# First layer of a hybrid decoder trunk: the first four pairs of w_in tiles computed together, input features outermost

## The chip, the cores and the metric

The kernel runs on one core of one Trainium2 chip. The metric is the device time of one execution, in microseconds (us): the median of several runs of the same program. The engines are TensorE (PE for its matmuls, PEld for its weight loads), VectorE (DVE), ScalarE (ACT), GpSimd (POOL) and SyncE (SP), which issues nearly all transfers. "mm" below is one matmul instruction of 128 x 128 weights against 256 columns, unless another size is given.

## The reference, cut to what matters

Two layers; each has an RMSNorm, one input projection, three token mixers, gates, an output projection and a feed-forward part. The change touches only the start of layer 0: the norm and the first part of `h @ w_in`.

```python
def reference(x, mix_norm, w_in, ...):          # x (1, 256, 1024), w_in (2, 1024, 5892)
    for l in range(DEPTH):                       # DEPTH = 2
        h = _rmsnorm(x, mix_norm[l])
        proj = (h @ w_in[l]).astype(jnp.float32)
        ret_c, fox_c, rwkv_c, gate_c = jnp.split(proj, splits, axis=-1)
        ...
        y_rwkv = _rwkv7_branch(rwkv_c, ...)      # the first four pairs of tiles feed this branch
        ...
        x = x + merged @ w_out[l]
        ...
```

## The kernel before

Activations lie transposed: 128 input features on the partitions, 256 tokens along the row, so x is eight blocks of 128 x 256, loaded as four tiles `x0_0` to `x0_3` of two blocks each. A weight tile is 128 input features by 128 output features, and a **pair** is two output tiles: 2 x 8 weight blocks, one megabyte in `in_win`. All products are computed in two parts: a weight or an activation is split into a rounded part (`whi`, `xh`) and the rest (`wlo`, `xl`), and each block costs three mm: whi by xh, whi by xl, wlo by xh (`mm3`, L285 to L294). So a pair is 48 mm, and four pairs are 192.

**Weights.** `weights` lists the weight transfers in the order in which they are used. `_piece` (L251) takes the next one: SP transfers it into `raw` (three buffers), ACT makes `whi` of eight blocks (L273, a cast of 128 x 1024), DVE makes `wlo` (L274). `whi` and `wlo` have four buffers each; a transfer into `raw` waits until DVE has made the last `wlo` out of that buffer. `refill` stays some pieces ahead of TensorE.

**The start.** TensorE first runs 30 matmuls on a tile of zeros (`pz`, L170). SP issues x0_0, the parameters, half of the first weights, x0_1, the other half, x0_2, x0_3, then the second weights, the constants and so on. `norm_add` (L392, L393) scales each x tile by the norm's gain and splits it; the rest of the norm, one factor for each token, is applied to the results. `layer` calls it for all four x tiles, with pieces of weights between.

**The first four pairs.** `gemm_halves` with a cut of 7 computes pair 0 (all but the last input block of both tiles first), then `gemm_pair` computes pairs 1, 2 and 3, each over all eight input blocks before the next begins. The sum of squares (`norm_sum`, L403 to L407) ends in `rstd`, whose matmul `pn` (L419) stands between pairs 1 and 2 and whose small DVE chain leads to `dg`; `replicate` (matmul `pss`, L429) spreads the factor and stands between pairs 2 and 3. `rwkv_in` multiplies each pair by the factor (`pj`, L642), takes the difference of neighbouring tokens on POOL (`dd`, L644) and mixes (L633) into r, k, v and wg.

**After them.** Two generators, one of the matmuls and one of the RWKV steps, are interleaved by a table of weights (`PACE`); the scheduler orders each engine's instructions by priority. The next matmuls are `mqk` (L437 to L439, 48 of 512 columns) and `mv` (48 of 260 columns). The first RWKV step loads `lora` (L668, 256 KB), and the matmuls `pw` and `pa` (L673, L674) read it with `xw` (L663) and wg. Engines run their instructions in order.

Of the kernel before, what the change touches and what calls it, by code (L numbers as in the profile page):

```python
# [8 lines left out]
F32 = mybir.dt.float32  # L9
# [82 lines left out]
def pack_inputs(inp, depth=DEPTH):  # L92
    f = {k: np.asarray(v) for k, v in inp.items()}
    out = {}

    def fm(a, n):
        return a.reshape(n, P).T

    out["xt"] = np.ascontiguousarray(f["x"][0].T.reshape(KT, P, T).transpose(1, 0, 2))
    out["const"] = np.concatenate([CONSTS[k] for k in C_ORDER], 1)  # L100
    pr = []
    for l in range(depth):
        fb = np.broadcast_to(f["fox_f_bias"][l][None, :], (P, 4))
        cols = {
            "mixg": fm(f["mix_norm"][l], 8), "ffng": fm(f["ffn_norm"][l], 8), "mu": fm(f["rwkv_mu"][l], 8),
            "w0": fm(f["rwkv_w0"][l], 2), "a0": fm(f["rwkv_a0"][l], 2), "kk": fm(f["rwkv_k_k"][l], 2),
            "ka": fm(f["rwkv_k_a"][l], 2), "rk": fm(f["rwkv_r_k"][l], 2), "rgn": fm(f["rwkv_gn"][l], 2),
            "retgn": fm(f["ret_gn"][l], 2),
            "fq": np.tile(f["fox_q_norm"][l], 2)[:, None], "fk": np.tile(f["fox_k_norm"][l], 2)[:, None],
            "fb": fb, "w2a2": np.concatenate([f["rwkv_w2"][l], f["rwkv_a2"][l]], 0), "g2": f["rwkv_g2"][l],  # L110
        }
        pr.append(np.concatenate([cols[k] for k, _ in PARAMS], 1))
    out["par"] = np.ascontiguousarray(np.stack(pr))

    def tiles(w, cols, nk):
        return w[:, cols].reshape(nk, P, -1, P).transpose(1, 2, 0, 3)

    R, F, W, G = 0, 1024, 1024 + 772, 1024 + 772 + 1024
    order = np.concatenate([
        np.arange(W, W + 1024),  # L120
        np.arange(R, R + 512), np.arange(R + 768, R + 1024)])
    win, wqk, wv, wgt = [], [], [], []
    for l in range(depth):
        w = f["w_in"][l]
        t = tiles(w, order, KT)
        win.append(t.reshape(P, N_IN, 2, KT, P).transpose(1, 0, 2, 3, 4).reshape(N_IN, P, 2 * KT * P))
        wqk.append(w[:, F:F + 512].reshape(KT, P, 512).transpose(1, 0, 2).reshape(P, KT * 512))
        vf = w[:, F + 512:F + 772].reshape(KT, P, 260).transpose(1, 0, 2).reshape(P, KT * 260)
        vr = w[:, R + 512:R + 768].reshape(KT, P, 256).transpose(1, 0, 2).reshape(P, KT * 256)
        wv.append(np.concatenate([vf, vr], 1))  # L130
        wgt.append(tiles(w, np.arange(G, G + 3 * DM), KT).reshape(P, 3, 4, 2 * KT * P).transpose(1, 2, 0, 3))
    out["wqk"] = np.ascontiguousarray(np.stack(wqk))
    out["win"] = np.ascontiguousarray(np.stack(win))
    out["wgate"] = np.ascontiguousarray(np.stack(wgt))
    out["wv"] = np.ascontiguousarray(np.stack(wv))
    pp, wo, wg, wd = [], [], [], []
    for l in range(depth):
        pp.append(np.stack([tiles(f[n][l], np.arange(DM), 2).reshape(P, 2 * DM) for n in ("p_ret", "p_fox", "p_rwkv")]))
        wo.append(tiles(f["w_out"][l], np.arange(DM), KT).reshape(P, 4, 2 * KT * P).transpose(1, 0, 2))
        gu = tiles(f["w_gate_up"][l], np.arange(2 * DFF), KT).reshape(P, 2, FT // 2, 2 * KT * P)  # L140
        wg.append(gu.transpose(2, 1, 0, 3))
        wd.append(tiles(f["w_down"][l], np.arange(DM), FT).transpose(1, 0, 2, 3).reshape(4, 2, P, FT, P)
                  .transpose(0, 2, 1, 3, 4).reshape(4, P, 2 * FT * P))
    out["pp"] = np.ascontiguousarray(np.stack(pp))
    out["wo"] = np.ascontiguousarray(np.stack(wo))
    out["wg"] = np.ascontiguousarray(np.stack(wg))
    out["wd"] = np.ascontiguousarray(np.stack(wd))
    return out


class Kernel:
    def __init__(self, ctx, tc, d, depth=DEPTH, debug=None):
        self.tc, self.nc, self.d, self.depth = tc, tc.nc, d, depth
        self.debug = debug or {}
        nc = self.nc
        e = ctx.enter_context
        self.cp = e(tc.tile_pool(name="cp", bufs=1))
        self.raw = e(tc.tile_pool(name="raw", bufs=3))
        self.spl = e(tc.tile_pool(name="spl", bufs=4))
        self.xp = e(tc.tile_pool(name="xp", bufs=4))  # L160
        self.ps = e(tc.tile_pool(name="ps", bufs=4, space=bass.MemoryType.PSUM))
        self.dr = e(tc.tile_pool(name="dr", bufs=1, space=bass.MemoryType.DRAM))
        self.uid = 0


        zero = self.cp.tile([P, T], mybir.dt.bfloat16, name="zero")
        nc.vector.memset(zero, 0.0)
        pz = self.ps.tile([P, T], F32, tag="fr", bufs=2, name="pz")
        for _ in range(30):
            nc.tensor.matmul(pz, zero[:, 0:P], zero, start=True, stop=True)  # L170
        par = [self.cp.tile([P, P_RES], F32, name=f"par{l}") for l in range(depth)]

        self.pad(self.xp, 16)
        self.xt = [self.xp.tile([P, 2, T], F32, tag="x", bufs=5, name=f"x0_{j}") for j in range(4)]
        nc.sync.dma_start(self.xt[0], d["xt"][:, 0:2, :])
        nc.sync.dma_start(par[0], d["par"][0, :, 0:P_RES])
        self.jobs, self.raws, self.ready, self.cur = list(self.weights()), [], [], []
        w0 = self.raw.tile([P, 2080], F32, tag="raw", name=self.nm("raw"))
        for j in range(4):
            if j:  # L180
                nc.sync.dma_start(self.xt[j], d["xt"][:, 2 * j:2 * j + 2, :])
            if j < 2:
                nc.sync.dma_start(w0[:, 1024 * j:1024 * (j + 1)], d["win"][0, 0, :, 1024 * j:1024 * (j + 1)])
        self.jobs[0:1] = [(w0, 4, P, 0), (w0, 4, P, 4), (w0, 8, P, 8)]
        self.par = par
        self.con = con = self.cp.tile([P, C_RES], F32, name="con")
        self.identb, self.maskb = zero[:, 0:P], zero[:, P:]
        self.c = {}
        for k, (o, n) in C_OFF.items():
            if k in FETCHED:  # L190
                continue
            v = con[:, o:o + n]
            if k in C_SHAPE:
                v = v.rearrange("p (a b) -> p a b", a=C_SHAPE[k][0])
            self.c[k] = v
        cc = self.c["cc"]
        self.cc = lambda i: cc[:, i:i + 1]
# [24 lines left out]
    def weights(self):  # L222

        d = self.d
        for l in range(self.depth):
            for j in range(N_IN):
                yield d["win"][l, j], 16, P, 0
                if j == 3:
                    for k in (0, 4):
                        yield d["wqk"][l, :, k * 512:(k + 4) * 512], 4, 512, 0  # L230
                    yield d["wv"][l, :, 0:KT * 260], KT, 260, 0
            yield d["wv"][l, :, KT * 260:], KT, 256, 0
            for b in range(3):
                for c in range(4):
                    yield d["wgate"][l, b, c], 16, P, 0
                for bb in ((), (0, 1), (2,))[b]:
                    yield d["pp"][l, bb], 16, P, 0
            for j in range(4):
                yield d["wo"][l, j], 16, P, 0
# [68 lines left out]
    def gemm_halves(self, xs, kcut=None, hook=None, tag="mm"):  # L308
# [14 lines left out]
        for lo, hi in ((0, kcut), (kcut, n)):  # L323
# [3 lines left out]
            if hook and not lo:  # L327
                hook()
        return ps

    @staticmethod
    def run(gen):
# [130 lines left out]
    def layer(self, l):  # L463
        tc, nc, d = self.tc, self.nc, self.d
        if l == 0:
            self.norm_start(0, "mixg")
            for j in range(4):
                self.norm_add(j, False)
                if j != 2:
                    self.piece()  # L470
        xs = self.xs
        with ExitStack() as st:
            e = st.enter_context
# [22 lines left out]
    def mixers(self, l, xs):  # L496
        self.y = [None] * 3
        self.mx = []
        self.need = None
        ps = [self.gemm_halves(xs, 7, tag="rw")]  # L500
        if l == 0:
            self.load_rest()
        for _ in range(1):
            ps.append(self.run(self.gemm_pair(xs)))
        rn, dg = self.rstd()
        ps.append(self.run(self.gemm_pair(xs)))
        rstd = self.replicate(dg)
        rw = self.rwkv_in(l, xs, rstd, ps)
        clock = {"gemm": 0.0, "rwkv": 0.0}
        run = {"gemm": self.gemms(l, xs, rstd, rn), "rwkv": self.rwkv(l, rw)}  # L510
# [686 lines left out]
```

## Time and profile before

| | us |
|---|---|
| median of 3 runs (799.79 to 800.15) | 800.09 |
| the profiled execution's own time | 800.76 |
| its span, first to last instruction | 799.0 |
| TensorE busy with matmuls (7018 of them) | 783.6 (98%) |
| VectorE busy | 576.2 (72%) |
| ScalarE busy | 397.1 (50%) |
| GpSimd busy | 61.6 (8%) |

The span lies inside the profiled execution's time, which is 0.67 us above the median. A timeline row gives the start, the length, the engine, the line, the operation, output and inputs; matmuls overlap in the array, so the step from one start to the next is what one costs. A bracket at its end is the time that the engine stood idle before it, and what ended that.

### The profile page before, as it was taken

How to read it: one execution, taken by the hardware profiler on the slowest of the kernel's cores; microseconds unless marked ns; L12 is line 12 of the kernel's file. 1: busy time of each engine (PE TensorE's matmuls, PEld its weight loads, DVE VectorE, ACT ScalarE, POOL GpSimd, SP SyncE). 2: the span in 40 equal slices, each digit the busy share in tenths (PEclk: the TensorE clock that was granted, in tenths of full speed). 3: DMA queues.
4: the chain of work that ended last, by engine and by line, in shares of the span. 5: the costliest groups of instructions: out<-in, count | busy, mean ns of one | idle time of the engine just before them, and what ended most of it. 6: DMA issues, size and time to landing. Idle time of an engine off the chain costs nothing.

```text
span 799.0 us, 16543 instructions
## 1 busy us (share of the span) xinstructions
PE 783.6 (98%) x7018; PEld 762.5 (95%) x7018; DVE 576.2 (72%) x900; ACT 397.1 (50%) x543; POOL 61.6 (8%) x83
## 2 busy tenths in 40 slices
PE   8999899999999999999999999999999999999998
PEld 6999899999999999999998988999999999999997
DVE  5897979597867666656678798877878666666453
ACT  6367445535645444445444764554456545444331
POOL 3201210031000000000023030101110000000000
PEclk9999999999999999999999999999999999999999
DMA  8565524335454554556554553452445454555650
GB/s 308 208 226 167 170 80 169 140 114 205 161 208 167 203 205 172 191 184 211 200 188 175 197 172 106 162 174 106 142 176 190 180 201 174 206 202 164 211 190 27
DMA packets 27802, 140.42 MB, mean 176 GB/s; under 512 B 7600, under 2 KB 9168, under 8 KB 12496
## 3 DMA queue, kind: packets, MB, share of 16 engines
q1 hardware_dynamic: 27728, 139.36, 50.2%
q8 instruction: 55, 0.90, 0.5%
q14 instruction: 19, 0.16, 0.1%
HBM read 136.97 MB, written 1.33 MB: 173 GB/s over the span
## 4 chain that ended last, share of the span: by engine, by line
PE 88%; DVE 6%; DMA 2%; ACT 1%; issue 1%; POOL 1%; SPq 0%; POOLq 0%; DVEq 0%; ACTq 0%
PE mm L290 26%; PE mm L294 25%; PE mm L293 25%; DVE wlo L274 2%; PE mqk L439 1%; PE mqk L438 1%; PE mqk L437 1%; ACT whi L273 1%; DMA rsw<-rqk 1%; PE pgm L762 1%; DVE rkk L745 1%; DMA raw<-in_win 1%; DMA raw<-in_pp 1%; PE mv L437 1%; PE mv L439 1%
## 5 line engine op out<-in xcount | busy, mean ns | idle before, releaser
L273 ACT CAST whi<-raw 128x1024 fp32r<-128x1024 f32 (+1 forms) x257 | 264.7, 1033 | 321.7 <-PE mm L293 232.2
L274 DVE TENSOR_TENSOR wlo<-raw,whi 128x1024 fp32r<-128x1024 f32 (+1 forms) x257 | 313.3, 1221 | 143.0 <-ACT whi L273 142.3
L290 PE MATMUL mm<-xh,whi 128*128 128x256 f32 x1312 | 368.0, 280 | 0.5 <-ACT whi L273 0.5
L294 PE MATMUL mm<-xh,wlo 128*128 128x256 f32 x1248 | 346.3, 277 | 0.7 <-DVE wlo L274 0.7
L293 PE MATMUL mm<-xl,whi 128*128 128x256 f32 x1248 | 346.3, 278 | 0.0
L290 PEld LDWEIGHTS mm<-xh,whi 128*128 128x128 f32 x1312 | 246.6, 188 | 2.8 <-issue 0.9
L294 PEld LDWEIGHTS mm<-xh,wlo 128*128 128x128 f32 x1248 | 234.4, 188 | 1.1 <-DVE wlo L274 0.9
L293 PEld LDWEIGHTS mm<-xl,whi 128*128 128x128 f32 x1248 | 234.5, 188 | 0.8 <-issue 0.5
L290 PE MATMUL mm<-hi,whi 128*128 128x256 f32 x576 | 160.1, 279 | 0.0
L294 PE MATMUL mm<-hi,wlo 128*128 128x256 f32 x544 | 150.9, 277 | 0.0
L293 PE MATMUL mm<-lo,whi 128*128 128x256 f32 x544 | 150.8, 277 | 0.0
L290 PEld LDWEIGHTS mm<-hi,whi 128*128 128x128 f32 x576 | 108.2, 188 | 0.6 <-issue 0.3
L294 PEld LDWEIGHTS mm<-hi,wlo 128*128 128x128 f32 x544 | 102.1, 188 | 0.2
L293 PEld LDWEIGHTS mm<-lo,whi 128*128 128x128 f32 x544 | 102.1, 188 | 0.1
L569 POOL TENSOR_TENSOR gate<-gate,gate 128x512 f32<-128x512 f32 x10 | 13.3, 1336 | 142.3 <-DVE gate L567 142.3
L600 DVE TENSOR_TENSOR h<-t,mm 128x512 f32<-128x512 f32 x22 | 15.1, 687 | 11.5 <-PE mm L294 8.6
L567 DVE SCALAR_TENSOR_TENSOR gate<-gate,mm 128x512 f32<-128x512 f32 x24 | 16.1, 682 | 8.6 <-PE mm L294 8.5
L597 DVE TENSOR_TENSOR t<-mm,rstd 128x512 f32<-128x512 f32 (+1 forms) x24 | 15.2, 645 | 8.5 <-PE mm L294 8.5
L553 DVE TENSOR_TENSOR gate<-mm,rstd 128x512 f32<-128x512 f32 x24 | 16.5, 689 | 3.8 <-PE mm L294 3.5
L293 PE MATMUL mm<-xh,wlo 128*128 128x256 f32 x64 | 18.0, 281 | 0.7 <-DVE wlo L274 0.7
L439 PE MATMUL mv<-whi,xl 128*128 128x260 f32 (+1 forms) x64 | 18.6, 290 | 0.0
L437 PE MATMUL mv<-whi,xh 128*128 128x260 f32 (+1 forms) x64 | 18.6, 290 | 0.0
(259 smaller groups left out, 797.9 us busy)
## 6 DMA issues: line engine op xcount, KB each, us to landing
raw<-in_wg SPq DMA_DIRECT2D x44, 1024.0 KB, 4.7
raw<-in_wgate SPq DMA_DIRECT2D x24, 1024.0 KB, 4.8
raw<-in_wd SPq DMA_DIRECT2D x16, 1024.0 KB, 5.0
raw<-in_win SPq DMA_DIRECT2D x13, 1024.0 KB, 8.0
raw<-in_wo SPq DMA_DIRECT2D x8, 1024.0 KB, 4.8
raw<-in_pp SPq DMA_DIRECT2D x6, 1024.0 KB
raw<-in_wd SPq DMA_DIRECT2D x8, 768.0 KB, 4.3
raw<-in_wqk SPq DMA_DIRECT2D x4, 1024.0 KB, 5.0
```

The costliest lines, as they stand in the source:

```text
L273: nc.scalar.copy(hi[:, :m * width], r)
L274: nc.vector.tensor_tensor(out=lo[:, :m * width], in0=r, in1=hi[:, :m * width].bitcast(F32), op=ALU.subtract)
L290: nc.tensor.matmul(out, wh, xh, start=first, stop=False)
L293: nc.tensor.matmul(out, wh, xl, start=False, stop=False)
L294: nc.tensor.matmul(out, wl, xh, start=False, stop=last)
L437: nc.tensor.matmul(out, xh[:, s], wh, start=first, stop=False)
L439: nc.tensor.matmul(out, xl[:, s], wh, start=False, stop=last)
L553: nc.vector.tensor_tensor(out=g, in0=ps, in1=self.b2(rstd), op=ALU.mult)
L567: nc.vector.scalar_tensor_tensor(out=g, in0=g, scalar=1.0, in1=ps, op0=ALU.add, op1=ALU.mult)
L569: (nc.vector if bb == 2 and c >= 1 else nc.gpsimd).tensor_tensor(out=m, in0=m, in1=g, op=ALU.add)
L597: nc.vector.tensor_tensor(out=t[:, o, :], in0=p, in1=self.bs(rstd, o), op=ALU.mult)
L600: nc.vector.tensor_tensor(out=h, in0=t, in1=pu, op=ALU.mult)
```

## The change

The first four pairs of layer 0 get a function of their own, `first_pairs`. It holds four results at once (pairs 0 and 1 in the PSUM tiles of tag "rw", 2 and 3 in those of "mm") and goes over the input features in four steps kk of two blocks each; in each step it does all four pairs: 4 x 2 x 2 blocks, 48 mm. The weights of these pairs have a layout of their own, `win0`: one megabyte for each step kk, in the order of use. The other pairs stay in `win`.

Of the first megabyte, ScalarE's queue issues the first quarter (256 KB), ahead of the load of its activation table; SP issues x0_0, the parameters, the second quarter, the other half, then x0_1, the second megabyte, x0_2, the third, x0_3. The fourth megabyte and the constants follow. The x tile of step kk+1 is split while step kk is computed. `rstd` is called after pair 0 of the last step, `replicate` after pair 2 of the last step. The matmuls on zeros are 22 instead of 30. Layer 1 does what it did.

```diff
-        for _ in range(30):
+        for _ in range(22):
             nc.tensor.matmul(pz, zero[:, 0:P], zero, start=True, stop=True)
...
+        w = [self.raw.tile([P, 2080], F32, tag="raw", name=self.nm("raw")) for _ in range(3)]
+        nc.scalar.dma_start(w[0][:, 0:512], d["win0"][0, :, 0:512])
         nc.sync.dma_start(self.xt[0], d["xt"][:, 0:2, :])
         nc.sync.dma_start(par[0], d["par"][0, :, 0:P_RES])
-        w0 = self.raw.tile([P, 2080], F32, tag="raw", name=self.nm("raw"))
-        for j in range(4):
-            if j:
-                nc.sync.dma_start(self.xt[j], d["xt"][:, 2 * j:2 * j + 2, :])
-            if j < 2:
-                nc.sync.dma_start(w0[:, 1024 * j:1024 * (j + 1)], d["win"][0, 0, :, 1024 * j:1024 * (j + 1)])
-        self.jobs[0:1] = [(w0, 4, P, 0), (w0, 4, P, 4), (w0, 8, P, 8)]
+        nc.sync.dma_start(w[0][:, 512:1024], d["win0"][0, :, 512:1024])
+        nc.sync.dma_start(w[0][:, 1024:2048], d["win0"][0, :, 1024:2048])
+        for j in range(1, 4):
+            nc.sync.dma_start(self.xt[j], d["xt"][:, 2 * j:2 * j + 2, :])
+            if j < 3:
+                nc.sync.dma_start(w[j][:, 0:2048], d["win0"][j])
+        self.jobs[0:3] = [(w[0], 4, P, 0), (w[0], 4, P, 4), (w[0], 8, P, 8), (w[1], 16, P, 0), (w[2], 16, P, 0)]
...
+    def first_pairs(self, xs):
+        ps = [self.ps.tile([P, 2, T], F32, tag=t, bufs=n, name=self.nm("mm")) for t, n in (("rw", 2), ("rw", 2), ("mm", 4), ("mm", 4))]
+        for kk in range(4):
+            if kk < 3:
+                self.norm_add(kk + 1, False)
+            if kk == 2:
+                self.load_rest()
+            for j in range(4):
+                if kk == 3 and j == 1:
+                    rn, dg = self.rstd()
+                if kk == 3 and j == 3:
+                    rstd = self.replicate(dg)
+                for m in range(2):
+                    for k in range(2 * kk, 2 * kk + 2):
+                        if not self.cur:
+                            self.refill()
+                        self.mm3(ps[j][:, m, :], self.block(), xs[k], k == m == 0, k == KT - 1 and m == 1)
+        return ps, rn, rstd
...
             self.norm_start(0, "mixg")
-            for j in range(4):
-                self.norm_add(j, False)
-                if j != 2:
-                    self.piece()
+            self.norm_add(0, False)
+            self.piece()
...
-        ps = [self.gemm_halves(xs, 7, tag="rw")]
         if l == 0:
-            self.load_rest()
-        for _ in range(1):
-            ps.append(self.run(self.gemm_pair(xs)))
-        rn, dg = self.rstd()
-        ps.append(self.run(self.gemm_pair(xs)))
-        rstd = self.replicate(dg)
+            ps, rn, rstd = self.first_pairs(xs)
+        else:
+            ps = [self.gemm_halves(xs, 7, tag="rw"), self.run(self.gemm_pair(xs))]
+            rn, dg = self.rstd()
+            ps.append(self.run(self.gemm_pair(xs)))
+            rstd = self.replicate(dg)
```

What the scheduler makes of it is seen at three places. First, TensorE where its early work goes on from one weight transfer to the next. Before, at the step from pair 0 (mm_170, mm_171) to pair 1 (mm_230), whose first weights are whi_174 and wlo_175:

```order
L294 MATMUL mm_170<-xl_150,whi_139 128x256
L290 MATMUL mm_171<-xh_149,whi_155 128x256
L293 MATMUL mm_171<-xh_149,wlo_156 128x256
L294 MATMUL mm_171<-xl_150,whi_155 128x256
L290 MATMUL mm_230<-xh_123,whi_174 128x256
L293 MATMUL mm_230<-xl_124,whi_174 128x256
L294 MATMUL mm_230<-xh_123,wlo_175 128x256
L290 MATMUL mm_230<-xh_123,whi_174 128x256
```

Now, at the step from kk = 0 to kk = 1 (the pairs are mm_141 to mm_144; xh_120 is the first x tile, xh_145 the second; whi_159 and wlo_160 come from the second megabyte):

```order
L298 MATMUL mm_144<-xh_120,whi_155 128x256
L301 MATMUL mm_144<-xl_121,whi_155 128x256
L302 MATMUL mm_144<-xh_120,wlo_156 128x256
L298 MATMUL mm_141<-xh_145,whi_159 128x256
L301 MATMUL mm_141<-xl_146,whi_159 128x256
L298 MATMUL mm_142<-xh_145,whi_159 128x256
L301 MATMUL mm_142<-xl_146,whi_159 128x256
L302 MATMUL mm_141<-xh_145,wlo_160 128x256
L298 MATMUL mm_141<-xh_145,whi_159 128x256
```

Before, the first mm on the second transfer's wlo is the third of pair 1, with 142 of the 192 mm still to do from it on; now it is the fifth of step kk = 1, with 140 to do.

Second, TensorE around `pw` and `pa`. Before they stand right behind the last of the 48 mqk:

```order
L439 MATMUL mqk_489<-whi_490,xl_150 128x512
L673 MATMUL pw_594<-xw,lora_511 128x256
L674 MATMUL pa_595<-wg_399,lora_511 128x256
L673 MATMUL pw_594<-xw,lora_511 128x256
L674 MATMUL pa_595<-wg_399,lora_511 128x256
L437 MATMUL mv_615<-whi_515,xh_123 128x260
```

Now they stand within the mv matmuls, with 23 of these ahead of them:

```order
L466 MATMUL mv_607<-whi_506,xh_145 128x260
L467 MATMUL mv_607<-wlo_507,xh_145 128x260
L699 MATMUL pw_585<-xw,lora_502 128x256
L700 MATMUL pa_586<-wg_450,lora_502 128x256
L699 MATMUL pw_585<-xw,lora_502 128x256
L700 MATMUL pa_586<-wg_450,lora_502 128x256
L468 MATMUL mv_607<-whi_506,xl_146 128x260
```

The matmul `pss`, which was between pairs 2 and 3, now stands behind the fifth mqk, so behind all four pairs; `pn` stands behind pair 0 of the last step, 36 mm before their end. From the place where `pg` (L685) stood on, some 360 rows into TensorE's list, the rows are the same in both.

Third, SP's queue where `lora` is loaded. Before it is behind raw_645, which reuses the buffer of raw_449, from which DVE makes its last wlo as wlo_491, behind the mix of k:

```order
L263 DMA raw_547<-in_win 128x2048
L780 DMA ti<-in_const 128x128
L263 DMA raw_645<-in_win 128x2048
L668 DMA lora_511<-in_par 128x512
L263 DMA raw_721<-in_win 128x2048
```

Now there is one more weight transfer ahead of it, raw_712, which reuses the buffer of raw_504; the last wlo out of that is wlo_523, at the same place in DVE's list, behind the mix of k:

```order
L271 DMA raw_538<-in_win 128x2048
L806 DMA ti<-in_const 128x128
L271 DMA raw_636<-in_win 128x2048
L271 DMA raw_712<-in_win 128x2048
L694 DMA lora_502<-in_par 128x512
L271 DMA raw_789<-in_wv 128x2048
```

The transfer of `lora` is still the one right behind the transfer that waits for DVE's second wlo after the factor, but the work on DVE that it waits for comes after the four pairs, not beside pair 3.

## Rows read from the trace of the kernel before

**Rows 1.** The page, part 1: engine, busy us, share, instructions.

```profile
PE 783.6 (98%) x7018; PEld 762.5 (95%) x7018; DVE 576.2 (72%) x900; ACT 397.1 (50%) x543; POOL 61.6 (8%) x83
```

**Rows 2.** Waits of TensorE from 7 to 34 us, longest: total us, times, longest.

```profile
PE mm L293 <- DVE wlo L274: 0.7, 2, 0.4
```

**Rows 3.** Timeline of TensorE at the stage's turning points.

```profile
7.67 0.39 PE L290 MATMUL mm<-xh,whi 128*128 128x256 f32 x1 [0.46 <-ACT whi L273]
...
16.65 0.39 PE L294 MATMUL mm<-xh,wlo 128*128 128x256 f32 x1 [0.66 <-DVE wlo L274]
16.87 0.28 PE L290 MATMUL mm<-xh,whi 128*128 128x256 f32 x1
...
28.08 0.59 PE L429 MATMUL pss<-dg,con 128*128 128x256 f32 x2
...
34.16 0.39 PE L437 MATMUL mqk<-whi,xh 128*128 128x512 f32 x1
...
45.34 0.48 PE L673 MATMUL pw<-xw,lora 64*128 64x256 f32 x1
```

**Rows 4.** Windows: stretch, length, busy by engine, granted clock, DMA share, GB/s.

```profile
0.00:5.40 5.40, 4.35 (x21) 3.10 (x22) 0.63 (x3) 2.31 (x3) 4.51 (x19) 1.00 0.55 151
5.40:7.30 1.90, 1.80 (x11) 1.12 (x9) 0.17 (x1) 0.30 (x1) 0.87 (x3) 1.00 0.95 277
7.30:8.00 0.70, 0.34 (x1) 0.19 (x1) 0.35 (x1) 0.70 (x3) 0.00 (x0) 1.00 1.01 407
8.00:10.70 2.70, 2.08 (x13) 1.64 (x12) 2.51 (x6) 2.70 (x7) 0.00 (x0) 1.00 1.06 387
```

**Rows 5.** Timeline of ScalarE and VectorE over the start.

```profile
7.00 0.62 ACT L273 CAST whi<-raw 128x512 fp32r<-128x512 f32 x1 [1.94 <-DMA raw<-in_win]
...
8.44 0.91 ACT L392 ACTIVATE xh<-x,par 128x256 fp32r<-128x256 f32 x2
...
11.79 0.62 ACT L406 ACTIVATE sq<-x 128x512 f32<-128x512 f32 x1
...
14.29 1.98 ACT L273 CAST whi<-raw 128x1024 fp32r<-128x1024 f32 x2
...
15.37 2.36 DVE L274 TENSOR_TENSOR wlo<-raw,whi 128x1024 fp32r<-128x1024 f32 x2 [0.25 <-ACT whi L273]
```

**Rows 6.** Timeline of TensorE's matmuls on zeros, whole and in cuts.

```profile
1.05 6.15 PE L170 MATMUL pz<-zero 128*128 128x256 bf16 x30 [1.05 <-DVE zero L167]
...
5.50 0.64 PE L170 MATMUL pz<-zero 128*128 128x256 bf16 x2
...
5.72 0.63 PE L170 MATMUL pz<-zero 128*128 128x256 bf16 x2
...
6.82 0.38 PE L170 MATMUL pz<-zero 128*128 128x256 bf16 x2
```

**Rows 7.** Timeline of ScalarE and VectorE behind the token factor.

```profile
29.11 0.36 ACT L431 COPY rstd<-pss 128x256 f32<-128x256 f32 x1
...
30.38 1.35 DVE L642 TENSOR_TENSOR pj<-mm,rstd 128x256 f32<-128x256 f32 x3
...
37.17 1.21 DVE L274 TENSOR_TENSOR wlo<-raw,whi 128x1024 fp32r<-128x1024 f32 x1
...
40.99 0.42 ACT L663 ACTIVATE xw<-wg 64x256 f32<-64x256 f32 x1 [2.80 <-DVE wg L633]
```

**Rows 8.** SP's queue around the load of lora; then windows as in 4.

```profile
38.41 0.33 SPq L263 DMA_DIRECT2D raw<-in_win  x1
...
38.79 0.42 SPq L668 DMA_DIRECT2D lora<-in_par  x1
...
43.20:43.60 0.40, 0.40 (x3) 0.33 (x2) 0.40 (x3) 0.40 (x1) 0.00 (x0) 1.00 0.14 51
```

**Rows 9.** Timeline of VectorE and TensorE before and at TensorE's next wait.

```profile
69.01 0.17 DVE L345 TENSOR_SCALAR z<-pnk 128x8 f32<-128x8 f32 x1 [2.28 <-PE pnk L359]
...
87.36 1.12 PE L748 MATMUL pb<-rkk,con 128*128 128x512 f32 x2 [1.46 <-DVE rkk L745]
```

More of the change, by code (lines that the diff above doesn't have):

```diff
@@ L132, in pack_inputs @@
     out["wqk"] = np.ascontiguousarray(np.stack(wqk))
-    out["win"] = np.ascontiguousarray(np.stack(win))
+    head = win[0][:4].reshape(4, P, 2, 4, 2 * P)
+    out["win0"] = np.ascontiguousarray(head.transpose(3, 1, 0, 2, 4).reshape(4, P, 16 * P))
+    out["win"] = np.ascontiguousarray(np.concatenate([win[0][4:]] + win[1:]))
     out["wgate"] = np.ascontiguousarray(np.stack(wgt))
@@ L174, in __init__ @@
         self.xt = [self.xp.tile([P, 2, T], F32, tag="x", bufs=5, name=f"x0_{j}") for j in range(4)]
+        self.jobs, self.raws, self.ready, self.cur = list(self.weights()), [], [], []
+        w = [self.raw.tile([P, 2080], F32, tag="raw", name=self.nm("raw")) for _ in range(3)]
+        nc.scalar.dma_start(w[0][:, 0:512], d["win0"][0, :, 0:512])
         nc.sync.dma_start(self.xt[0], d["xt"][:, 0:2, :])
         nc.sync.dma_start(par[0], d["par"][0, :, 0:P_RES])
-        self.jobs, self.raws, self.ready, self.cur = list(self.weights()), [], [], []
-        w0 = self.raw.tile([P, 2080], F32, tag="raw", name=self.nm("raw"))
-        for j in range(4):
-            if j:
-                nc.sync.dma_start(self.xt[j], d["xt"][:, 2 * j:2 * j + 2, :])
-            if j < 2:
-                nc.sync.dma_start(w0[:, 1024 * j:1024 * (j + 1)], d["win"][0, 0, :, 1024 * j:1024 * (j + 1)])
-        self.jobs[0:1] = [(w0, 4, P, 0), (w0, 4, P, 4), (w0, 8, P, 8)]
+        nc.sync.dma_start(w[0][:, 512:1024], d["win0"][0, :, 512:1024])
[5 more added lines that the diff above has]
+        self.jobs[0:3] = [(w[0], 4, P, 0), (w[0], 4, P, 4), (w[0], 8, P, 8), (w[1], 16, P, 0), (w[2], 16, P, 0)]
         self.par = par
@@ L226, in weights @@
             for j in range(N_IN):
-                yield d["win"][l, j], 16, P, 0
+                if l or j > 3:
+                    yield d["win"][l * N_IN + j - 4], 16, P, 0
+                else:
+                    yield d["win0"][j], 16, P, 0
                 if j == 3:
@@ L499, in mixers @@
         self.need = None
-        ps = [self.gemm_halves(xs, 7, tag="rw")]
         if l == 0:
-            self.load_rest()
-        for _ in range(1):
+            ps, rn, rstd = self.first_pairs(xs)
+        else:
+            ps = [self.gemm_halves(xs, 7, tag="rw"), self.run(self.gemm_pair(xs))]
+            rn, dg = self.rstd()
             ps.append(self.run(self.gemm_pair(xs)))
-        rn, dg = self.rstd()
-        ps.append(self.run(self.gemm_pair(xs)))
-        rstd = self.replicate(dg)
+            rstd = self.replicate(dg)
         rw = self.rwkv_in(l, xs, rstd, ps)
```

## The prediction

> **What bounds the kernel now.** I read the page's busy times first: TensorE is busy 98% of the span [rows 1], so nothing can be gained but time in which it has no real work, and nothing can be lost but by giving it such time. Next the waits of TensorE by stage: behind 17 us it has next to none until 87.36 [rows 9], so the start is where the change acts. There the timeline shows three things. The first real mm begins at 7.67, behind the cast of the first weights [rows 3], which itself waited for their transfer until 7.00 [rows 5]. Then there are gaps, on wlo above all [rows 2, 3]; the last one ends at 16.65. From 16.87 to the first mqk at 34.16 it never stops: 141 mm with pn and pss among them in 17.29 us, 0.12 us each [rows 3]. So four pairs end 26.5 us after they began, where 192 x 0.12 = 23.0 would do.
>
> **What the start gains.** A fixed number of mm is left behind the last gap, so the end of the stage is set by when that gap ends and how many are left. Before: 16.65, with 142 to go (the order in the section on the change). Now the gap that I expect to end last is the fifth mm of step kk = 1, the first on wlo_160, with 140 to go. When does it end?
>
> By bytes: x0, par and the first two quarters are 0.81 MB, with the other half 1.33, with x1 1.60, with the second megabyte 2.64. The windows of before [rows 4] sum to 0.815 MB at 5.4, 1.34 at 7.3, 1.63 at 8.0 and 2.67 at 10.7 us. Landing comes later than the mean count, since the slowest of the DMA engines decides: the first 0.5 MB of weights was in the count at 5.4 and was cast at 7.00 [rows 4, 5], 1.6 us. Two things pull forward: the transfers' share is only 0.55 up to 5.4 [rows 4], while one queue issues one thing after another, and two queues fill more of that; and x2 and x3, two of the transfers with short rows, now come behind the second megabyte. I take 0.8 us for both and 1.3 for the lag, so the second megabyte is there at 10.6 - 0.8 + 1.3 = 11.1; without the head start and with the full lag at 12.2. The other half of the first megabyte comes at about 8.1.
>
> By ScalarE: from 8.1 it has one cast (0.99), two xh (0.91), two squares (0.62 each) before it can cast whi_159 [rows 5]: 11.2. So this cast starts at about 11.3; DVE's wlo starts 1.08 behind the cast's start and takes 1.23 (2.36 for two) [rows 5]: 13.6, and TensorE goes on at 13.65. If the transfer lands at 12.2 it is 14.55; with all of ScalarE's inputs 0.3 earlier 13.35. TensorE itself comes to this place at about 13.3 (second quarter at 6.7, cast to 7.3, 20 mm to 9.8, a short wait for wlo_156 to 10.2, 26 mm), so it waits 0.3 and is not itself the bound. Behind it each step kk takes 48 x 0.12 = 5.8 us of TensorE, and a step's 1.3 MB take 3.3 us at 387 to 407 GB/s [rows 4], its ScalarE work 3.5 (two casts, two xh, a square) and its DVE work 4.1: no further gap. The **gain at the start** is 16.65 - 13.65 + 2 x 0.12 = 3.2 us, with 2.3 and 3.6 as its ends.
>
> **What costs nothing.** ScalarE issues one transfer (SP's take 0.33 to 0.43 [rows 8]) before any data are there; its cover is the wait for them, without which it would be 0.4. The constants come behind the fourth megabyte: 5.8 MB at 0.39 to 0.41 MB/us is 19 us, and pn needs them at 26. The new layout has the same bytes and 8 KB rows. Eight zero matmuls less take 22 x 0.213 from 1.05: they end at 5.74, before the first operands are all split (about 6); what else hangs on them is a rival, below.
>
> **What it costs behind the pairs.** All four pairs now end before the token factor is there. Let E be the end of the pairs: 34.16 - 3.2, and 0.4 less since pss (0.59, half hidden [rows 3]) now stands behind it: 30.55. pss comes behind five mqk of 0.233 (48 in 11.2 us [rows 3]), so at E + 1.2; with its 0.6 and the copy's 0.36 [rows 7] the first pj starts at E + 2.3. Before, DVE took from 30.38 to 38.38 for pj, mix and two wlo, until the wlo that frees a buffer for the next megabyte [rows 7]; the same list now ends at E + 10.3. Before, SP issued that megabyte at 38.41 and lora right behind it, and lora's last bytes moved up to 43.6 [rows 8]: 5.2 us. So now lora is there at E + 15.5 = 46.05. TensorE comes to pw at 45.34 - 3.2 + 23 x 0.12 (the mv now ahead of it) = 44.9. Before it came at 45.34 and lora had been there for 1.7 us. So a **new wait of 1.1 us** stands at pw, and all mv and mm queued behind it on TensorE wait as well. It is 0 if DVE's list is a microsecond shorter than before, and 2.0 if DVE's wlo ahead of pj, whose cast waits for E, holds it up by another. xw is not the bound: 11.0 us from pj to its end [rows 7] gives 43.9. Nor is the PSUM that mv takes over from pairs 2 and 3: the last pj ends at E + 11.0, mv starts at E + 11.6.
>
> From there TensorE's list is the old one. DVE waits 2.28 us for TensorE ahead of 69.01, and the wait of 1.46 at 87.36 comes out of a chain that starts there [rows 9], so it moves with TensorE. The RWKV chain is 0.7 later at pw and wanted 2.1 earlier, 2.8 against these 2.28 and smaller idle times before: at most 0.5 is lost, and I take 0.
>
> **Sum.** 3.2 - 1.1 = 2.1 us, 800.76 - 2.1 = 798.7 for an execution like the profiled one; its 0.67 above the median of the runs taken off, **798.0**.
>
> **The rivals.** *No new wait* (lora in time): 3.2, 796.9. For it: 1.1 us is small beside an 8 us list on DVE; against: the same list before held no idle time but 0.6 us for POOL. *A late second megabyte or a longer wait*: 2.2 - 1.1 = 1.1, or 3.2 - 2.0 = 1.2: 799.0, within 0.2%; for it, the slow 277 GB/s up to 7.3 at a share of 0.95 [rows 4], which more queues can't mend. That is also what is left if the change doesn't do what it says, and the first weights come no earlier by the second queue. The Trainium skill (DMA: Bandwidth & Descriptors, "Issuing engines are not separate DMA queues") says just this: transfers started by several engines share the same 16 DMA engines, and only the issue time is saved. By it my 0.8 would be 0.5 (the moved x tiles) and the gain 2.9, the sum 798.3; the share of 0.55 speaks for some room.
>
> *A late clock*, which ends on the other side. TensorE's zero matmuls start 0.21 apart at 5.50 and 5.72, the 1.2 GHz level for 256 columns, and about 0.11 apart at the end [rows 6], the 2.4 GHz level; 30 in 6.15 us put the rise at about 6.6, after 5.5 us without a pause. (The column of the granted clock reads 1.00 all along; the steps decide.) Now the unbroken stretch ends at 5.74, and a wait for the second quarter follows. If the clock rises late, at R, each us of busy TensorE until then loses 0.45 (0.213 against 0.12). From 7.3 on it is busy, and 0.6 of it hides in its waits. At R = 13 the gain of 2.1 is gone (5.7 x 0.45 = 2.6), from R = 17 it is slower by over 0.2%, at 18 the loss is 4.2: 802. Against: the work before 6.6 is nearly as dense as it was, and before the clock held through a wait of 0.66 us [rows 3]. The Trainium skill (TensorE: Matmul & The Clock Gate, "What's actually happening") says that the throttled state is the default and activity releases it; by that rule the fewer zeros bring a risk that the row of before can't show, since there they outlast the rise.
>
> **How the numbers follow.** Forecast 0.60, no new wait 0.15, late transfer or longer wait 0.20, late clock 0.05. A run of this kernel tells 0.2% (1.6 us) from no change: under 798.49 is faster. The forecast's own ends reach across that (gain at the start 2.3, or wait 2.0), so about 0.17 of its 0.60 falls within. Faster: 0.43 + 0.15 = 0.58; same: 0.17 + 0.20 = 0.37; slower 0.05. The range leaves out the slow clock and the upper part of the late cases above, and gains beyond 3.2 below: 796.9 to 799.5.
>
> **What would show it.** First real mm between 5.7 and 6.5, four of them, a gap to about 7.3, a last gap on wlo_160 ending at 13.4 to 14.5; first mqk at 30 to 31.5; a gap ahead of pw at 45 to 46, released by lora's transfer and not by ScalarE or DVE. Wrong would be: a step of 0.21 between mm behind 8 us; a gap at wlo of steps kk = 2 or 3; no gap at pw.

## The result

The forecast was 798.0 us. The changed kernel takes **803.62 us** (median of 8 runs, 801.36 to 804.75) against 799.94 (8 runs) for the kernel before: a ratio of 1.0044, 95% interval 1.0034 to 1.0055. It is slower by 3.7 us by the medians, where 2 us less were forecast, and outside the range of 796.9 to 799.5.

The profiled execution took 803.62, its span is 801.7. The page's first part is nearly that of before [rows 1]: the same work, 8 matmuls fewer.

```profile
PE 783.3 (98%) x7010; PEld 762.9 (95%) x7010; DVE 576.5 (72%) x899; ACT 396.8 (49%) x543; POOL 62.0 (8%) x83
```

Not even the sum of busy time tells that something went wrong: the matmuls that ran at half the clock (below) count as busy. The waits of TensorE from 4 to 75 us do tell it (engine, line, operation, who was waited for; total us, times, longest):

```profile
PE mm L298 <- DVE fn L1005: 2.5, 1, 2.5
PE pw L699 <- DMA lora<-in_par: 1.3, 1, 1.3
PE mm L298 <- ACT xh L421: 0.7, 1, 0.7
PE mm L298 <- ACT whi L281: 0.5, 1, 0.5
PE mm L301 <- DVE xl L422: 0.3, 1, 0.3
```

The gaps on wlo [rows 2, 3] are gone. The second line is the wait that was forecast. The first one wasn't. TensorE's timeline at the turning points, to be read against [rows 3]:

```profile
5.90 0.39 PE L298 MATMUL mm<-xh,whi 128*128 128x256 f32 x1 [0.69 <-ACT xh L421]
...
7.69 0.56 PE L298 MATMUL mm<-xh,whi 128*128 128x256 f32 x1 [0.45 <-ACT whi L281]
8.05 0.42 PE L301 MATMUL mm<-xl,whi 128*128 128x256 f32 x1
8.27 0.42 PE L302 MATMUL mm<-xh,wlo 128*128 128x256 f32 x1
...
14.96 0.28 PE L302 MATMUL mm<-xh,wlo 128*128 128x256 f32 x1
...
31.44 0.39 PE L466 MATMUL mqk<-whi,xh 128*128 128x512 f32 x1
...
32.71 0.67 PE L458 MATMUL pss<-dg,con 128*128 128x256 f32 x2
...
47.39 0.45 PE L699 MATMUL pw<-xw,lora 64*128 64x256 f32 x1 [1.28 <-DMA lora<-in_par]
...
54.20 0.36 PE L298 MATMUL mm<-xh,whi 128*128 128x256 f32 x1 [2.48 <-DVE fn L1005]
...
90.77 1.13 PE L774 MATMUL pb<-rkk,con 128*128 128x512 f32 x2 [1.45 <-DVE rkk L771]
```

The first mqk begins 2.72 us earlier (34.16 to 31.44). pw, which had no wait, stands 2.05 later than before (45.34 to 47.39), and behind mv the first mm waits 2.48 for fn. Who is late? The token factor's copy, the first pj and fn (the normalized q and k, which VectorE makes out of mqk), on ScalarE and VectorE:

```profile
33.42 0.37 ACT L460 COPY rstd<-pss 128x256 f32<-128x256 f32 x1 [0.84 <-PE pss L458]
...
33.82 1.29 DVE L668 TENSOR_TENSOR pj<-mm,rstd 128x512 f32<-128x512 f32 x2
...
53.37 1.29 DVE L1005 TENSOR_TENSOR fn<-mqk,y 128x512 f32<-128x512 f32 x2
```

rstd comes 4.31 later than at 29.11, the first pj 3.44 later than at 30.38 [rows 7]. The kernel before has fn and that mm at

```profile
51.12 1.29 DVE L979 TENSOR_TENSOR fn<-mqk,y 128x512 f32<-128x512 f32 x2
...
53.25 0.28 PE L290 MATMUL mm<-xh,whi 128*128 128x256 f32 x1
```

so it had 1.45 us to spare between the end of the first fn (the row holds two; the first ends at 51.80) and the matmul that takes over the PSUM tile which this fn reads. In the changed kernel fn is 2.25 later, TensorE 1.53 earlier (without the wait it would be there at 51.72): 2.25 + 1.53 - 1.45 = 2.33 of wait, 2.48 measured.

Last, two windows of the changed kernel (columns as in [rows 4]):

```profile
7.80:11.10 3.30, 3.30 (x16) 3.30 (x17) 1.69 (x2) 2.20 (x4) 0.00 (x0) 0.50 0.98 372
55.50:58.95 3.45, 3.45 (x15) 3.09 (x14) 0.63 (x2) 0.49 (x2) 0.00 (x0) 0.51 0.62 183
```

The granted clock is at its lower level, 1.2 GHz, in both: 16 matmuls in 3.3 us, where 0.12 us each would make 27. The first stretch follows gaps of 0.69, 0.32 and 0.45 us, the second the gaps of 1.28 and 2.48.

**The account**, from the first mqk to pb, TensorE's next wait for VectorE (1.46 at 87.36 [rows 9], 1.45 at 90.77 now): 53.20 us before, 59.33 after, so 6.13 more. pss among the mqk costs 0.62 (its two neighbours start 0.43 and 0.19 later than the step of 0.23), pw 1.28, the mm behind mv 2.48, and the second slow stretch some 1.6 (a size that the first experiment gives, by comparing two executions): 5.98 of the 6.13. Less the 2.72 of the start, 3.41 are left at pb, and the profiled spans differ by 2.7.

### The profile page after: what moved, and what is told of

Read it like the earlier page. It is cut to its first block, busy times and chain, and to the rows that moved or that the text cites. A ratio compares the mean times of both kernels' runs of the same rounds, so it can differ in the third digit from the quotient of the medians.

```text
span 801.7 us, 16531 instructions
## 1 busy us (share of the span) xinstructions
PE 783.3 (98%) x7010; PEld 762.9 (95%) x7010; DVE 576.5 (72%) x899; ACT 396.8 (49%) x543; POOL 62.0 (8%) x83
## 4 chain that ended last, share of the span: by engine, by line
PE 86%; DVE 8%; DMA 2%; issue 1%; POOL 1%; ACT 1%; SPq 1%; POOLq 0%; DVEq 0%; ACTq 0%
PE mm L298 26%; PE mm L302 25%; PE mm L301 25%; DVE wlo L282 3%; DMA rsw<-rqk 1%; PE pgm L788 1%; ACT whi L281 1%; DVE rkk L771 1%; DMA raw<-in_win 1%; POOL lo L406 1%; DVE ttmp L847 0%; PE mqk L468 0%; PE mqk L467 0%; PE mqk L466 0%; PE pu L905 0%
## 5 line engine op out<-in xcount | busy, mean ns | idle before, releaser
L301 PE MATMUL mm<-xl,whi 128*128 128x256 f32 x1264 | 351.8, 278 | 0.3 <-DVE xl L422 0.3
L302 PE MATMUL mm<-xh,wlo 128*128 128x256 f32 x1264 | 351.4, 278 | 0.0
L301 PEld LDWEIGHTS mm<-xl,whi 128*128 128x128 f32 x1264 | 238.8, 189 | 1.4 <-DVE xl L422 0.5
L302 PEld LDWEIGHTS mm<-xh,wlo 128*128 128x128 f32 x1264 | 238.4, 189 | 0.2
L467 PE MATMUL mv<-wlo,xh 128*128 128x260 f32 (+1 forms) x64 | 18.3, 287 | 0.0
```

The lines of the kernel that those rows point to most:

```text
L301: nc.tensor.matmul(out, wh, xl, start=False, stop=False)
L302: nc.tensor.matmul(out, wl, xh, start=False, stop=last)
L467: nc.tensor.matmul(out, xh[:, s], wl, start=False, stop=False)
```

## The experiments

The theory was now that **the token factor is late**: it is computed behind the new loop of four pairs, VectorE's chain from it is late as a whole, both waits are ends of this chain, and the slow clock follows from them. Its rivals: the fall of the clock at the start (fewer zeros) is the loss; or each wait has a cause of its own, the lora transfer and the PSUM tile. All times are medians; ratios are to the kernel before on the same chip.

**30 zeros in the changed kernel.**

```
-        for _ in range(22):
+        for _ in range(30):
```

> The changed kernel with the 30 matmuls of zeros that the kernel before has, in place of 22; nothing else. In the changed kernel the granted clock falls to 1.2 GHz from 7.8 to 11.1 us, and its matmuls take 0.213 us there. Theory 1 (the loss lies later: the gap of 1.28 us at pw, the gap of 2.48 us at the first mm behind mv, and the slow stretch of about 1.7 us behind them): the eight zeros keep the clock, or they don't, but either way the stretch up to 31 us gains at most 1 us, pw and the mm behind mv wait as long or longer (1.3 to 2, 2.5 to 3), and the time is 802.5 to 804. Theory 2 (the fall at the start is the loss): with the zeros back the time is 800 or less.

Measured: 801.88 us, ratio 1.0033 [1.0021, 1.0045]. The time is lower than expected and far from the rival's 800. In the profiled execution (801.38) both waits stand as they were, but the clock held in both windows. Its waits of TensorE:

```profile
PE mm L298 <- DVE fn L1005: 2.6, 1, 2.6
PE pw L699 <- DMA lora<-in_par: 1.2, 1, 1.2
```

its windows, and its TensorE at the places that are compared:

```profile
7.80:11.10 3.30, 2.70 (x22) 2.60 (x22) 1.42 (x2) 2.36 (x5) 0.00 (x0) 1.00 1.01 413
55.50:58.95 3.45, 3.45 (x29) 3.34 (x28) 1.18 (x5) 1.85 (x4) 0.00 (x0) 1.00 0.66 192
...
31.36 0.39 PE L466 MATMUL mqk<-whi,xh 128*128 128x512 f32 x1
...
54.14 0.35 PE L298 MATMUL mm<-xh,whi 128*128 128x256 f32 x1 [2.56 <-DVE fn L1005]
...
89.08 1.13 PE L774 MATMUL pb<-rkk,con 128*128 128x512 f32 x2 [1.45 <-DVE rkk L771]
```

That sizes the two slow stretches, as far as two executions can. At the start: the first mqk begins at 31.36 here and at 31.44 there, so between these two the slow clock from 7.8 us cost 0.1; the one with the fast clock waited longer instead, for whi until 8.40 and for wlo until 11.65. Later: from the mm behind mv (54.14 here, 54.20 there) to pb (89.08, 90.77) it is 34.94 against 36.57 us, 1.6 for the second. The five executions show a step of that size: 801.38, 801.53 and 801.88 have a mean granted clock of 1.000, 803.18 and 803.64 one of 0.998. So whether the clock falls seems to differ between executions of one kernel; the mean does not tell where it fell in the two. Nor is it shown that eight zeros at the start have a part in whether it falls 50 us later.

**22 zeros in the kernel before.**

```
-        for _ in range(30):
+        for _ in range(22):
```

> The kernel before with 22 matmuls of zeros in place of 30; nothing else. Theory 1: the last gap of its start, the one on wlo that ends at 16.87 us, is set by transfers and casts, so a slower clock ahead of it is hidden; the time stays within 0.5 us of the kernel before (799.5 to 800.5). Theory 2 (fewer zeros let the clock fall, and that is the whole of the loss of 3.7 us): the granted clock falls behind the zeros here too and the time is 802.5 to 804.

Measured: 801.31 us (12 runs, 798.93 to 802.95), ratio 1.0015 [1.0006, 1.0024]. Neither theory's number. In the profiled execution, the longest of the twelve, the granted clock from 7.10 to 15.00 us is

```profile
7.10:15.00 7.90, 6.74 (x27) 5.95 (x28) 5.95 (x11) 5.58 (x12) 0.00 (x0) 0.54 1.01 392
```

with 27 matmuls where the kernel before has 44 in the same window, and the first mqk begins at 36.52, not 34.16. So in the old order the eight zeros are worth about 1.2 us by the ratio and 2.4, at this place, in this execution. The forecast took them as free in the new order. The pair of executions above agrees; two runs below (mv's tiles from another pool, and 30 zeros on top of the token factor forward) speak against it.

**Lora early.** The table's load moves behind the last megabyte of w_in, in layer 0 only.

```
             if kk == 2:
                 self.load_rest()
+                self.lora = self.t512("lora")
+                self.nc.sync.dma_start(self.lora.rearrange("p a t -> p (a t)"), self.d["par"][0, :, P_RES:])
...
-        lora = self.t512("lora")
-        nc.sync.dma_start(fl(lora), self.d["par"][l, :, P_RES:])
+        if l:
+            lora = self.t512("lora")
+            nc.sync.dma_start(fl(lora), self.d["par"][l, :, P_RES:])
+        else:
+            lora = self.lora
```

> The changed kernel with the lora table of layer 0 loaded right behind the last megabyte of w_in, some 15 us earlier; layers 1 to 3 as they are. The gap of 1.28 us at pw goes. Theory 1a (the chain of VectorE up to fn is what is late): TensorE comes to the first mm behind mv 1.3 us earlier and waits there 3.7 to 3.9 in place of 2.48, the clock may still fall behind it, and the time falls by at most 0.5, to 803 to 804. Theory 1b (each wait is a cost by itself): the mm behind mv waits 2.5 as in the changed kernel, and the time falls by 1.3 or more, to 802.3 or below.

Measured: 804.39 us, ratio 1.0057 [1.0045, 1.0069]: nothing gained. The waits of TensorE:

```profile
PE mm L298 <- DVE fn L1010: 2.0, 1, 2.0
PE pw L704 <- ACT xw L691: 2.0, 1, 2.0
```

With the table there, pw stands right behind mqk on TensorE's list, as in the kernel before, and now waits for xw, the other end of the same chain. The two waits sum to 4.0 us, against 3.8 in the changed kernel. The wait moved; only, it moved to pw's other input and not, as expected, to the mm behind mv.

**PSUM tiles of mv from another pool** (fr in place of mm, layer 0; the function that makes them gets the pool's name as an argument), so that the mm behind mv doesn't need fn.

```
-        pv = yield from self.gemm_n(260, xs)
+        pv = yield from self.gemm_n(260, xs, tag="mm" if l else "fr")
```

> The changed kernel with the two PSUM tiles of mv in layer 0 taken from the pool fr in place of the pool mm, so that the first mm behind mv doesn't need the tile of the first mqk, which VectorE's fn has to read first. Theory 1 (this wait and the slow clock behind it make most of the loss): the gap of 2.48 us goes, the gap of 1.28 at pw stays, and the time falls by 2.5 if the clock still falls to 1.2 GHz behind pw (801.1), by 4.2 if it holds (799.4). Rival (VectorE is late as a whole): the gap comes back at the next user of a PSUM tile or of VectorE's result, with 2 us or more, and the time stays above 802.5.

Measured: 800.93 us (11 runs, 798.92 to 804.83), ratio 1.0019 [1.0004, 1.0034], 2.0 less than the changed kernel's by the ratios. The gap of 2.48 is gone, that at pw stays (1.26), and the clock holds at 55.50 to 58.95 (mm 0.11 apart). From the first mqk to pb it takes 55.46 us in place of 59.33:

```profile
33.22 0.39 PE L466 MATMUL mqk<-whi,xh 128*128 128x512 f32 x1
...
88.68 1.12 PE L774 MATMUL pb<-rkk,con 128*128 128x512 f32 x2 [1.45 <-DVE rkk L771]
```

That is 3.9 less, near the 4.2 that were expected. The median, which is the profiled execution, shows less of it because its start came out worse: the first mqk begins at 33.22 and not at 31.44, since TensorE ran at half speed until 13.6 us (more on that below). So this wait, with the clock that falls behind it, is worth about 4 of the 6 us that are lost behind the pairs. The gap did not come back at a later place, as the rival in the expectation had it: up to pb VectorE's lateness costs TensorE time only where it waits at pw and at the reused PSUM tile.

**The token factor forward**, to where its inputs are ready within the new loop.

```
-                if kk == 3 and j == 1:
+                if kk == 2 and j == 3:
                     rn, dg = self.rstd()
-                if kk == 3 and j == 3:
+                if kk == 3 and j == 1:
                     rstd = self.replicate(dg)
```

> The changed kernel with the token factor moved forward among the four pairs: its column sums stand ahead of the last pair's third eighth of the work and its replication (pss) one pair into the last quarter, where the changed kernel has the sums one pair into the last quarter and the replication behind all four pairs. The tables, the zeros (22) and the PSUM pools are the changed kernel's. Theory 1a (VectorE's chain from the token factor over pj, the mixes, xw and fn is what is late, and the two waits are its two ends): rstd is ready by 28.5 instead of 33.9, fn ends some 3 us earlier, the wait at pw and the wait at the first mm behind mv fall to 1 us together or less, the clock holds behind them, and the time is 798 to 800. Rival (the waits have causes of their own, the transfer of lora and the PSUM tile): both stay within 0.5 of 1.28 and 2.48, and the time stays above 802.

Measured: **798.57 us**, ratio 0.9983 [0.9974, 0.9992]: two lines moved by two pairs turn the loss into a gain. The timeline of rstd, pj and fn:

```profile
27.47 0.37 ACT L460 COPY rstd<-pss 128x256 f32<-128x256 f32 x1 [1.25 <-PE pss L458]
...
28.81 1.28 DVE L668 TENSOR_TENSOR pj<-mm,rstd 128x512 f32<-128x512 f32 x2
...
49.64 1.29 DVE L1005 TENSOR_TENSOR fn<-mqk,y 128x512 f32<-128x512 f32 x2
```

and all waits of TensorE from 4 to 75 us:

```profile
PE mm L302 <- DVE wlo L282: 0.6, 1, 0.6
PE mm L301 <- DVE xl L422: 0.3, 1, 0.3
PE mm L298 <- ACT whi L281: 0.3, 1, 0.3
PE mm L298 <- ACT xh L421: 0.2, 1, 0.2
```

rstd is 5.95 earlier than in the changed kernel, fn 3.73, and behind the start TensorE waits nowhere until pb, which begins at 84.57, 2.79 before the kernel before. Lora's load, whose issue hangs on VectorE's list, comes in time by itself. The rival of two separate causes falls: neither the load of lora nor the pool was edited.

**Three kernels on top of it.** The first adds the 30 zeros, the second the PSUM tiles of mv, the third the early lora as well (the edits are those shown).

> The kernel of the run before (token factor forward) with 30 matmuls of zeros. Theory 1a: the clock holds at the start as it did in the changed kernel with 30 zeros, the gap on the first low halves is then 0.5 to 1 us, the zeros give at most 1 us, and the time is 797 to 799.5. If the zeros are worth more than the chain (theory 2), it is over 1.5 us below the run before.

> The kernel of the run before with the PSUM tiles of layer 0's mv in the pool fr besides. Theory 1a: if no wait of more than 0.3 us is left at the first mm behind mv, this changes nothing (within 0.5 us of the run before). Where one is left, it goes, and the time falls by its length.

> The kernel of the run before with the lora table of layer 0 loaded behind the last megabyte of w_in besides: all four edits together (token factor forward, 30 zeros, PSUM tiles of mv, early lora). Theory 1a: what is left at pw waits for xw, VectorE's and ScalarE's result, and not for the table, so the early table gives at most 0.5 us. If pw waits for the table alone, it gives the whole of the wait left there. The time expected is 796.5 to 798.5.

Measured: 797.39 us, 0.9972 [0.9961, 0.9983]; 797.63, 0.9969 [0.9959, 0.9978]; 797.40, 0.9966 [0.9953, 0.9978]. The second and third edits add nothing, as expected: where the chain is in time there is no wait for them to remove. The zeros make 1.2 us by the medians, 0.9 by the ratios; the intervals overlap, so this gain is likely, not shown.

**Filling the gap.** 20 matmuls nobody reads, between mv and the mm behind it, in the changed kernel (`self.filler` is the tile of zeros).

```
+        self.filler = zero
...
         pv = yield from self.gemm_n(260, xs)
+        if l == 0:
+            pf = self.ps.tile([P, T], F32, tag="fr", bufs=2, name=self.nm("pf"))
+            for _ in range(20):
+                nc.tensor.matmul(pf, self.identb, self.filler, start=True, stop=True)
```

> The changed kernel with 20 more matmuls of zeros and constants, whose result nobody reads, between the last matmul of mv and the first matmul behind it; on TensorE's list nothing else moves but pg, which comes forward to stand ahead of the last of them. They fill the gap of 2.48 us (20 matmuls at about 0.11 us are 2.2 us) and shorten nothing: fn still ends at about 54 us and the matmul behind still starts at about 54.2. If the slow stretch from 55.5 to 58.95 us is the price of the idle time, it goes and the time falls by 1.7 us, to about 802. If the slow stretch comes by itself, or costs nothing that is not waited for elsewhere, the time stays at 803.6.

Measured: 801.32 us, ratio 1.0022 [1.0011, 1.0032], 1.8 below the changed kernel by the ratios. The filler in TensorE's timeline:

```profile
51.44 2.25 PE L1014 MATMUL pf<-zero 128*128 128x256 bf16 x19
```

and the two windows of this execution:

```profile
7.80:11.10 3.30, 3.13 (x15) 3.13 (x16) 1.80 (x2) 2.30 (x5) 0.00 (x0) 0.52 1.04 418
55.50:58.95 3.45, 3.45 (x33) 3.45 (x32) 1.35 (x6) 2.93 (x7) 0.00 (x0) 1.00 0.56 188
```

fn ends no earlier (it begins at 53.32), the gap is filled with matmuls nobody reads (and with pg, which came forward), and yet the time falls by about what the slow stretch cost. The clock fell at the start here as well and held later. This speaks for the idle time as the cause of the second fall, but doesn't prove it. With 30 zeros the clock held once behind both waits, without a filler. Seven of the eleven executions here took 800.4 to 802.3 us, and four 803.2 to 803.5, about what the changed kernel takes; and since pg came forward and pb lost its wait of 1.45, the size may hold something of that order.

The Trainium skill (TensorE: Matmul & The Clock Gate, "HAM oscillation — how this bites in real kernels") tells of a kernel whose waits for data between bursts bring the slow clock back each time. The runs agree in part: the slow clock came back behind 1.28 and 2.48 us of waiting (3.45 us at 0.51), and with 30 zeros it held behind 1.21 and 2.56; the waits here are shorter than those of the Trainium skill's kernel.

**The late token factor alone**, in the kernel before: its sums one pair later and pss behind the fourth pair, old layout, old order of the pairs, 30 zeros.

```
-        rn, dg = self.rstd()
-        ps.append(self.run(self.gemm_pair(xs)))
+        if l == 0:
+            ps.append(self.run(self.gemm_pair(xs)))
+            rn, dg = self.rstd()
+            ps.append(self.run(self.gemm_pair(xs)))
+        else:
+            rn, dg = self.rstd()
+            ps.append(self.run(self.gemm_pair(xs)))
         rstd = self.replicate(dg)
```

> The kernel before, with its old weight layout, its 30 zeros and its order of the pairs, and only the token factor of layer 0 moved back by one pair: its column sums stand between the third and the fourth pair, its replication (pss) behind the fourth, right ahead of mqk, as in the changed kernel. Theory 1a: the late token factor alone makes the loss; rstd comes some 5 us later than at 29.11, pw waits 1 to 2.5 us for xw and the first matmul behind mv 1.5 to 3 us for fn, the granted clock may fall behind them, and the time is 802.5 to 805.5, 2.5 to 5.5 above the kernel before. Rival (the layout or the order of the new pairs makes it): the time stays within 1 us of the kernel before.

Measured: **803.97 us**, ratio 1.0049 [1.0036, 1.0062]. The waits of TensorE that are new:

```profile
PE mm L290 <- DVE fn L984: 2.3, 1, 2.3
...
PE pw L678 <- ACT xw L668: 0.7, 1, 0.7
```

and rstd, with the window in which the clock is down:

```profile
34.49 0.37 ACT L431 COPY rstd<-pss 128x256 f32<-128x256 f32 x1
...
55.50:58.95 3.45, 3.45 (x14) 3.11 (x14) 3.27 (x7) 1.33 (x3) 0.00 (x0) 0.52 0.25 91
```

The whole picture stands without the new layout, the new order and the fewer zeros: wait for fn, slow stretch behind it, 3.8 us lost. (The profiled execution, at 805.28, is one of the two longest of five.) rstd is at 34.49, 5.38 later than at 29.11. With the run that moves the factor forward, this is the experiment that decides: the late factor alone makes the loss, and the early one alone removes it.

**First weights on SyncE's queue again**, in the kernel with the token factor forward and 30 zeros.

```
-        nc.scalar.dma_start(w[0][:, 0:512], d["win0"][0, :, 0:512])
+        nc.sync.dma_start(w[0][:, 0:512], d["win0"][0, :, 0:512])
```

> The changed kernel with the token factor forward and 30 zeros, its first 256 KB of weights issued on SyncE's queue in the old manner, not on ScalarE's; nothing else. The issue on ScalarE lets the first transfers of x and of the parameters start one issue (about 0.6 us by the spacing of SyncE's issues) earlier. If that is on the path, the first real matmuls start 0.3 to 0.6 us later and the time is up to 0.6 above the 797.4 of the kernel with both; if the transfers of the first pairs are set by the total that moves, it is within 0.3 of it.

Measured: 796.92 us, ratio 0.9963 [0.9950, 0.9977], against 797.39 with the issue on ScalarE. No gain of the issue on ScalarE can be seen, but the two ratios' intervals overlap, and each reaches about 1 us to either side. The prediction's 0.8 us was for this head start and the moved x tiles together; by the rule that it weighed (the Trainium skill, DMA: Bandwidth & Descriptors, "Issuing engines are not separate DMA queues") the head start's part was 0.3. The runs fit that rule, but can't tell 0.3 us from nothing.

## Why the prediction was wrong

**The gain at the start**: right in kind, mis-sized. No gap on wlo is left, and the first mqk came at 31.44, within the 30 to 31.5 named. But E, the end of the pairs, was to be 30.55; it was 0.9 later, and pss in its new place took 0.62 and not 0.4. Of the 3.2 of the sum 2.72 - 0.62 = 2.1 are there, below the low end of 2.3. The step that failed is "waits 0.3 and is not itself the bound": TensorE is the bound. The place where it was to wait for wlo_160 until 13.65, with 140 mm to go, it reached at 14.96 and without a wait (the row above). With 30 zeros it was there at 14.81, again without a wait: its last gap had ended at 11.65, with 166 mm to go. Too early in the sum were the gaps within the first megabyte (forecast to end at 7.3 and 10.2, with 30 zeros at 8.40 and 11.65). In the changed kernel the first ended at 7.69, and 16 mm at the slow clock took the rest.

**The new wait at pw**: right. 1.1 forecast, 1.28 measured, released by lora's transfer; both ends came 1.2 to 1.3 us later than forecast (TensorE at 46.1, not 44.9), mostly because both hang on E. That xw is not the bound was right only with this transfer late: with it in time, pw waited for xw.

**"From there TensorE's list is the old one ... at most 0.5 is lost, and I take 0"**: this step failed, and it decides. It looked for the next place where the trace of before shows a wait, at 69.01 and 87.36 [rows 9], and the mm behind mv has none there, only 1.45 us to spare. The prediction had asked the very question for the PSUM that mv takes over ("mv starts at E + 11.6") and not for the next in the same ring: of the four buffers of the pool mm, pairs 2 and 3 hold one each, mqk takes the other two, mv takes over the pairs' two, and then the mm behind mv needs what mqk held until fn has read it. fn's chain starts at rstd like pj's, and VectorE's list from pj to fn was nearly full (15.40 of the 16 us from 31 to 47 in the kernel before). By the prediction's own rows pj was to come at E + 2.3 = 32.85, 2.47 later than before, fn with it, and TensorE earlier by 3.2 - 1.1 = 2.1: a wait of 2.47 + 2.1 - 1.45 = 3.1 us could have been estimated from the trace of before, and with it the sum, 2.1 - 3.1, is a loss of 1.0 before any fall of the clock. Measured were 2.48: pj came 3.44 later, fn only 2.25.

**The late clock**: the rival named the right direction and, for this execution, the wrong place. It was a late rise behind fewer zeros. In the profiled execution of the changed kernel the clock rose among the zeros (22 of them in 4.16 us; they ended at 5.21, not at 5.74) and fell again behind the gaps; steps of 0.21 between mm behind 8 us, named as a sign of being wrong, did come, and cost 0.1 us against the execution with 30 zeros. What cost 1.6 was a fall behind waits of which the forecast had put one there itself and should have put the other. The argument "before the clock held through a wait of 0.66 us" said nothing about 1.28 and 2.48. But the late rise is real too. The profiled execution with mv's tiles in the other pool, an edit that doesn't touch the start, has it. The zeros of the changed kernel:

```profile
1.05 4.16 PE L173 MATMUL pz<-zero 128*128 128x256 bf16 x22 [1.05 <-DVE zero L170]
```

and the zeros of that other kernel, with the place where its step falls from 0.21 to 0.12:

```profile
1.05 4.88 PE L173 MATMUL pz<-zero 128*128 128x256 bf16 x22 [1.05 <-DVE zero L170]
...
13.58 0.38 PE L302 MATMUL mm<-xh,wlo 128*128 128x256 f32 x1
13.80 0.29 PE L298 MATMUL mm<-xh,whi 128*128 128x256 f32 x1
```

There the 22 zeros all ran at the slow level (0.21 a step), so did the mm until 13.6, and the first mqk came 1.78 later than in the changed kernel's execution, near the 2.0 that the rival's own sum gives for a rise at 13.

**What costs nothing**: for eight zeros less this is not borne out. They cost 0.1 us at the start of the one pair of executions, 1.2 us in the order before, and likely about 1 us with the token factor forward. The one late rise seen in the new order, 1.78 us, came with 22 zeros; that 30 would have prevented it isn't shown. For the ScalarE issue no cost is seen, and no gain either.

## What to carry to other kernels

When an edit makes one engine earlier and moves a result later on another, walk down the list of the engine that gets ahead and take, for each buffer it takes over and each result it reads, the slack that the trace of before shows (releaser's end to taker's start), also where that trace shows no wait: the first slack smaller than the shift is the new bound. A factor that gates a whole chain of another engine belongs where its inputs are ready, not behind the loop that uses it: here two lines, moved by two pairs, were worth 5 us. Where a change puts new waits on TensorE, count with the slow stretch that may follow them: here 1.6 us behind 1.28 and 2.48.

## What was not expected of the hardware

Whether the clock falls seems to differ between executions of the same kernel: with 30 zeros in the changed kernel it held behind gaps of 1.21 and 2.56 us in the profiled execution; by the mean clock it held in three of five, and the time differs by some 1.8 us between the two kinds. The rise at the start differs too: among the kernels with 22 zeros the zeros took 4.05 to 4.88 us.

The granted clock's column can miss a slow stretch. In the execution with the late rise shown above it reads 1.00 from 7.80 to 11.10 us,

```profile
7.80:11.10 3.30, 2.38 (x11) 2.38 (x12) 1.40 (x2) 2.41 (x5) 0.00 (x0) 1.00 1.05 433
```

while its timeline shows 11 matmuls that follow one another at 0.21, the step of the 1.2 GHz level, two of them here:

```profile
10.17 0.41 PE L298 MATMUL mm<-xh,whi 128*128 128x256 f32 x1
10.38 0.41 PE L301 MATMUL mm<-xl,whi 128*128 128x256 f32 x1
```

The steps decide, as with the zeros of the kernel before [rows 6].
